# Norm 2's scales, one weight chunk's rounding and the last product's columns: three reorderings in a decoder block

## The chip, the cores and the metric

The kernel runs on one core of a Trainium2 chip. The metric is the device time of one execution in microseconds (us); lower is better. Engine names are those of the profile: PE multiplies matrices (PEld loads its weights), DVE, ACT and POOL work element by element, and SP is the queue from which most DMAs are issued.

## The reference

One decoder block on 512 positions of width 1024. Two token mixers run side by side and are merged by gates; then comes a SwiGLU channel mixer and a final norm. The change touches what follows the merge:

```python
m = jax.nn.sigmoid(z_ga) * y_a + jax.nn.sigmoid(z_gb) * y_b
x = x + m @ w_mix_out[l]                       # 1024 x 1024

h = rmsnorm(x, norm2_g[l])                     # "norm 2"
x = x + (jax.nn.silu(h @ ffn_w1[l]) * (h @ ffn_w3[l])) @ ffn_w2[l]   # 1024 -> 2816 -> 1024
return rmsnorm(x, norm_f_g)                    # final norm
```

## The kernel before

**Numbers in two parts.** Every product is made of float32r parts: an operand is split into a rounded high part (a cast on ACT, L133) and the rest as a low part (a subtraction on DVE or POOL, L129). One product is three matmuls: high by high, high by low, low by high. This split of a weight is called its *rounding* here.

**Weight chunks.** Weights come in a fixed list of chunks of up to 128 x 1024 (`chunks`). `load_chunk` issues the chunk's DMAs into one of four `raw` buffers, `emit_chunk` rounds it into one of five `hl` buffers, and `weights(key, ahead)` emits the list up to `ahead` chunks behind the one that is asked for (`AHEAD` is 4). Around the change the list reads: the last chunks of the mix matrix, then fb11_1, fb21_1, fb11_2, fb21_2, ft4_1, ft4_2 (quarters of ffn_w1 and ffn_w3 for the column pairs 1 and 2), then f1_0, f3_0, f1_1, f3_1 (pair 0, whole). The profile drops the numbers: fb11_2 is written from `raw_fb` to `hl_fb`, f3_0 from `raw_f` to `hl_f`.

**Seven products in place of eight.** The class `Sevenfold` multiplies by the mix matrix and by ffn_w2 in quarters, with sums of quarters in place of some of them. The output x is held as four row tiles of 128 positions, each in two halves of 512 columns: `x2[t][h]`. PE sums in PSUM banks (`bank`, `bank2`: 128 x 512 float32 each), r1, r2, r5 and r7, and `plus(t, h, b)` adds a bank to a half on DVE (L940). The steps at the end are `second` (products of the last index k; row tiles 0 and 1 are complete behind them) and `third(i, ks)` (the last products, into bank r1[i] once more, which complete row tile 2 + i).

**The end of the mix, `mix_end`.** Inside `manual_schedule` PE, ACT and DVE run in the order of the code. After `second` come six additions, then norm 2 for tiles 0 and 1: `rstd_begin` has squared the first-known half on ACT, `rstd_end` squares the other half, takes the root (ACT L562) and the reciprocal (DVE L563), and `scaled(t, h)` multiplies both halves by it (DVE L1100, into `xs`) and stores x to DRAM on the SP queue (`x2k`). PE then works off `third` in portions and, between them, transposes the scaled tiles in blocks of 128 columns (`turn_half`, PE L579): block c takes columns 128c to 128c + 127 of two row tiles, so blocks 0 to 3 need first halves only and blocks 4 to 7 second halves only. ACT makes the high part of each turned block (L582, h20h to h27h) and DVE the low part (L583). On the SP queue and POOL, pieces of later weights are loaded (L383), summed (`piece_sums`, L129 and L394) and stored (L398) in the same stretch.

**The start of the channel mixer.** The products for pairs 1 and 2 begin (PE L1211) on the turned columns of tiles 0 and 1. Tiles 2 and 3 are normalised meanwhile (`scaled(t, 0)`) and turned in between, blocks 4 to 7 first, and `fourth` multiplies by ft4 (L1255). When the last block is turned, banks are copied out (ACT L1241, L1259), the two SiLUs of `first` run (ACT L1221), and four more chunks are emitted.

**The end, `out_end`.** ffn_w2's product ends in the same steps. Each row tile is finished by the final norm: squares and a root on ACT (L555, L561, L562), a reciprocal on DVE, the multiplication by the norm's weights (DVE L1378), and the scale (L1388, L1390 on DVE, L1392 on ACT), then the DMAs to the output (L1395). For tiles 2 and 3 the last five products of `third` run in between (`rest`).

Outside `manual_schedule` the compiler's scheduler places instructions; `tc.issue_after(x)` holds them behind x.

Of the kernel before, what the change touches and what calls it, by code (L numbers as in the profile page):

```python
# [13 lines left out]
P = 128  # L14
# [82 lines left out]
def tile_block(ctx, tc, a, out):  # L97
# [449 lines left out]
    stats = consts.tile([P, 3 * NT, 3], F32, name="stats")  # L547
# [11 lines left out]
    def rstd_end(begun, half, junk):  # L559
        ss, r = begun  # L560
        act.activation(junk, half, AF.Square, accum_out=ss[:, 1:2])  # L561
        newest["root"] = act.activation(r, ss[:, 1:2], AF.Sqrt, scale=1.0 / D, bias=ss[:, 0:1]).ins  # L562
        vec.reciprocal(r, r)  # L563
        return r
# [385 lines left out]
    class Sevenfold:  # L950
# [35 lines left out]
        def product(self, banks, i, x_, w_, start, stop, again=False):  # L986

            (xh, xl), (wh, wl) = x_, w_
            ts = slice(i * P, (i + 1) * P)
            for n, (l_, r_) in enumerate(((xh, wh), (xh, wl), (xl, wh))):  # L990
                pe.matmul(banks[i], l_[:, ts], r_, start=start and n == 0, stop=stop and n == 2, skip_group_check=again)  # L991

        def run(self, sums, begun, end):
# [40 lines left out]
            def third(i, ks):  # L1034
                for k in ks:
                    self.product(r1, i, quarter(late[k][1], HI), *get(k, "t4"), False, k == kh - 1, True)

            for k in range(kh - 1):
                second(k, *get(k, "b22", "t2", "t3"))
                split_late()  # L1040
                if k == 0:
                    for i in range(2):
                        plus(i, 1, r5[i])
                        plus(2 + i, 1, r5[i])

            act.activation(warm, late[-1][1][0][:, :1].bitcast(F32), AF.Sqrt, scale=0.0, bias=eps_t)
            last = get(kh - 1, "b22", "t2", "t3", ahead=AHEAD - 1)
# [32 lines left out]
    def mix_end(second, plus, r1, r2, r7, third):  # L1080
        made = []

# [14 lines left out]
        def scaled(t, h):  # L1097
            r = rstd_end(begun[t], x2[t][h], sc[t][h])
            for i in range(2):
                newest["scaled"] = vec.tensor_scalar(out=sc[t][i], in0=x2[t][i], scalar1=r, scalar2=None, op0=ALU.mult).ins  # L1100
                nc.sync.dma_start(x2_kept[t][i][:, :], x2[t][i])


        with tc.manual_schedule(engines={ET.PE, ET.Activation, ET.DVE}):
# [7 lines left out]
            for t in range(2):  # L1112
                scaled(t, 1)
# [3 lines left out]
            for q in range(2):  # L1117
                turn_half("th", xs, "norm2_g", h2p, 0, [bank, bank2], range(4 * q, 4 * q + 4))
                for i in range(2):
                    third(i, [2 + q])  # L1120
# [14 lines left out]
            for t in (2, 3):  # L1135
                scaled(t, 0)
# [184 lines left out]
    with tc.issue_after(turned[0]), tc.issue_after(turned[1]):  # L1321
        for b in begun.values():
            b.first()
        emit_to(emitted[0] + 4)
        f_inputs()
# [46 lines left out]
    def finish(t, rest=None):  # L1372
# [13 lines left out]
        r = rstd_of([x2[t][h], x2[t][1 - h]], [bank2(f"jk{t}{i}") for i in range(2)], between)  # L1386

        vec.tensor_scalar(out=o[1 - h], in0=o[1 - h], scalar1=r, scalar2=None, op0=ALU.mult)  # L1388
        if t == 2:
            vec.tensor_scalar(out=o[h], in0=o[h], scalar1=r, scalar2=None, op0=ALU.mult)  # L1390
        else:
            act.activation(o[h], o[h], AF.Copy, scale=r)  # L1392

        for i in (1 - h, h):
            (nc.scalar if t == 3 and i == h else nc.sync).dma_start(o_nat[:, t, i * T : (i + 1) * T], o[i])  # L1395

    def out_end(second, plus, r1, r2, r7, third):
        kh, hold = outq.kh, 5
        second()
        for i in range(2):  # L1400
            plus(i, 1, r1[i])
            plus(i, 1, r2[i])
            plus(2 + i, 1, r1[i])
# [10 lines left out]
        for i in range(2):  # L1414

            def rest():
                third(i, range(kh - hold, kh))
                plus(2 + i, 0, r1[i])

            finish(2 + i, rest)  # L1420
# [35 lines left out]
```

## Time and profile before

| what | value |
|---|---|
| median of 3 runs | 799.59 us (799.19 to 799.9) |
| the profiled execution | 798.86 us |
| its span (first to last instruction) | 797.0 us |
| mean granted clock of PE | 0.998 |
| DMA | 188.13 MB, mean 236 GB/s |
| POOL busy | 360.2 us |
| PE's starts: mix product's end to first product of the channel mixer | 447 to 459 us |
| PE's last matmul begins | 789.91 us |

The span starts with the first instruction of the program. A row of a timeline gives the start, the time from the first start to the last end of the merged instructions, the engine, the line, the operation, output <- inputs, the shape and the count; in square brackets stands how long the engine was idle before it and what ended that. Starts of successive rows on PE and DVE overlap the ends of the earlier ones, since both engines are pipelined; how fast work goes through is read from the distance of the starts. A row of the waits gives the total, the number and the longest one. A row of the chain that ended last gives the start, the time, the engine and the line.

### The profile page before, as it was taken

The numbers are of one execution on the slowest core, as the hardware profiler recorded it, in microseconds if no ns is written. First come the engines' busy times: TensorE is split into PE (matmuls) and PEld (weight loads), VectorE is DVE, ScalarE is ACT, GpSimd is POOL, SyncE is SP. The second block draws the span as 40 slices with busy tenths as digits, with TensorE's granted clock in tenths as the row PEclk, the third lists the DMA queues.
The fourth block names the chain that finished last, engine by engine and source line by source line (L and its number), as shares of the span: only waits on it lengthen the run. The fifth ranks groups of instructions, "written<-read, shape, count | busy, mean of one in ns | idle before, by whom it ended". The sixth has DMA issues, their size and how long they took to land.

```text
span 797.0 us, 12582 instructions
## 1 busy us (share of the span) xinstructions
PE 786.5 (99%) x4374; PEld 688.8 (86%) x4374; DVE 695.8 (87%) x1097; ACT 472.6 (59%) x674; POOL 360.2 (45%) x347
## 2 busy tenths in 40 slices
PE   8999999999999999999999999999999999999996
PEld 7988888888888888888888797999999999888885
DVE  5799999999998997985899868898877798999956
ACT  7446688777679665562326466544455555556843
POOL 2576778788869988853350482113222221000000
PEclk9999999999999999999999999999999999999999
DMA  7746566577776786979987987588998898878652
GB/s 222 190 122 177 157 191 201 174 236 236 195 246 212 249 264 195 295 236 295 296 293 240 275 259 217 157 267 269 343 309 291 297 325 299 235 235 269 197 169 105
DMA packets 181074, 188.13 MB, mean 236 GB/s; under 512 B 14119, under 2 KB 142035, under 8 KB 181011
## 3 DMA queue, kind: packets, MB, share of 16 engines
q1 hardware_dynamic: 172195, 156.66, 63.8%
q0 software_dynamic: 8672, 30.41, 11.2%
q8 instruction: 34, 0.56, 0.3%
q10 hardware_dynamic: 144, 0.26, 0.1%
q14 instruction: 29, 0.24, 0.1%
HBM read 145.48 MB, written 38.80 MB: 231 GB/s over the span
## 4 chain that ended last, share of the span: by engine, by line
PE 95%; DVE 2%; ACT 1%; DMA 0%; issue 0%; SPq 0%; DVEq 0%
PE z L539 35%; PE fr L1211 24%; PE or L991 13%; PE yb L539 7%; PE ya L539 5%; PE mxr L991 4%; PE g L860 3%; PE f L539 2%; PE fr L1255 1%; DMA x<-in_x_dram 0%; DVE x L940 0%; PE z L632 0%; PE th L579 0%; PE tx L590 0%; DVE xs L1100 0%
## 5 line engine op out<-in xcount | busy, mean ns | idle before, releaser
L733 DVE SCALAR_TENSOR_TENSOR cv<-u,par,cv 128x511 f32<-128x511 f32 (+17 forms) x240 | 162.6, 728 | 1.1 <-ACT cv L730 0.9
L129 POOL TENSOR_TENSOR hl_in<-raw_in,hl_in 128x1024 fp32r<-128x1024 f32 x51 | 123.3, 2422 | 64.2 <-ACT hl_in L133 43.4
L129 POOL TENSOR_TENSOR fws<-fws 128x256 f32<-128x256 f32 x120 | 104.7, 875 | 75.1 <-DMA fws<-in_ffn_w_dram 69.5
L398 POOL DMA_DIRECT2D ot<-fwso x21 | 15.3, 731 | 166.1 <-DVE fwso L129 158.8
L1211 PE MATMUL fr<-hs_0h,hl_ft 128*128 128x256 f32 x320 | 59.2, 283 | 0.0
L133 ACT CAST hl_in<-raw_in 128x1024 fp32r<-128x1024 f32 x51 | 53.1, 1043 | 2.2 <-DMA raw_in<-in_w_in_dram 1.0
L129 DVE TENSOR_TENSOR hl_ft<-raw_ft,hl_ft 128x1024 fp32r<-128x1024 f32 x39 | 47.5, 1219 | 4.7 <-ACT hl_ft L133 4.7
L129 DVE TENSOR_TENSOR hl_fb<-raw_fb,hl_fb 128x1024 fp32r<-128x1024 f32 x30 | 36.9, 1231 | 15.9 <-ACT hl_fb L133 15.9
L1211 PEld LDWEIGHTS fr<-hs_0h,hl_ft 128*128 128x128 f32 x320 | 50.6, 192 | 0.0
L133 ACT CAST hl_ft<-raw_ft 128x1024 fp32r<-128x1024 f32 x40 | 41.6, 1047 | 12.4 <-PE fr L1211 9.2
L133 ACT CAST hl_fb<-raw_fb 128x1024 fp32r<-128x1024 f32 x30 | 31.5, 1050 | 24.4 <-PE fr L1211 11.6
L1211 PE MATMUL fr<-hs_0l,hl_ft 128*128 128x256 f32 x160 | 45.3, 283 | 0.0
L539 PE MATMUL z<-h10h,hl_in 128*128 128x512 f32 (+1 forms) x110 | 41.4, 378 | 0.0
L539 PE MATMUL z<-h11h,hl_in 128*128 128x512 f32 (+1 forms) x110 | 41.1, 376 | 0.0
L539 PE MATMUL z<-h17h,hl_in 128*128 128x512 f32 (+1 forms) x110 | 41.1, 376 | 0.0
L539 PE MATMUL z<-h13h,hl_in 128*128 128x512 f32 (+1 forms) x110 | 41.1, 376 | 0.0
L539 PE MATMUL z<-h14h,hl_in 128*128 128x512 f32 (+1 forms) x110 | 41.1, 376 | 0.0
L539 PE MATMUL z<-h15h,hl_in 128*128 128x512 f32 (+1 forms) x110 | 41.1, 376 | 0.0
L539 PE MATMUL z<-h16h,hl_in 128*128 128x512 f32 (+1 forms) x110 | 41.1, 376 | 0.0
L539 PE MATMUL z<-h12h,hl_in 128*128 128x512 f32 (+1 forms) x110 | 41.1, 375 | 0.0
L133 ACT CAST hl_ob<-raw_ob 128x1024 fp32r<-128x1024 f32 (+1 forms) x23 | 23.4, 1016 | 23.9 <-PE or L991 12.1
L394 POOL TENSOR_TENSOR fws<-fws 128x256 f32<-128x256 f32 x40 | 32.5, 813 | 2.8
(962 smaller groups left out, 2639.2 us busy)
## 6 DMA issues: line engine op xcount, KB each, us to landing
raw_in<-in_w_in_dram SPq DMA_DIRECT2D x52, 512.0 KB
fws<-in_ffn_w_dram SPq DMA_DIRECT2D x80, 256.0 KB
raw_ft<-fs SPq DMA_DIRECT2D x34, 512.0 KB
fs<-fws SPq DMA_DIRECT2D x23, 512.0 KB
ot<-fwso POOLq DMA_DIRECT2D x21, 512.0 KB, 5.8
fwso<-in_ffn_w_dram POOLq DMA_DIRECT2D x40, 256.0 KB, 7.3
fs<-fws POOLq DMA_DIRECT2D x17, 512.0 KB, 5.0
raw_ob<-in_ffn_w_dram SPq DMA_DIRECT2D x33, 256.0 KB
```

The lines of the kernel that those rows point to most:

```text
L129: return eng.tensor_tensor(out=o, in0=x, in1=y, op=ALU.subtract)
L133: copy(h, full)
L394: eng.tensor_tensor(out=q11, in0=q22, in1=q11, op=ALU.add)
L398: return queue.dma_start(dest, raw.rearrange("p (m n) -> p m n", m=dest.shape[1]))
L539: pe.matmul(ps, l, r, start=i == 0, stop=i == n - 1)
L733: vec.scalar_tensor_tensor(out=acc[c][:, s:], in0=u[c][:, : T - s], scalar=dw(c, s), in1=acc[c][:, s:], op0=ALU.mult, op1=ALU.add)
L860: pe.matmul(ps, l, r, start=k == 0, stop=k == len(mms) - 1)
L991: pe.matmul(banks[i], l_[:, ts], r_, start=start and n == 0, stop=stop and n == 2, skip_group_check=again)
L1211: pe.matmul(ps[:, HALVES[i]], lw[:, c, :], rx_, start=not (again or i or c or m), stop=bool(i and c == 3 and m == 2), skip_group_check=True,)
L1255: pe.matmul(self.r4[:, HALVES[i]], lw, rx_, start=not (i or c or m), stop=bool(i and c == 3 and m == 2), skip_group_check=True)
```

## The change

Five edits:

1. In the mix product the weight chunks are asked for one less ahead, so that fb11_2 is not rounded there. Its load is issued at the start of `mix_end`, ahead of the piece loads, and its rounding stands behind the first four transposed blocks.
2. `scaled` takes two row tiles. Both get their first half scaled, then both their second half. The second tile's root and reciprocal stand ahead of its first half's scale, as before.
3. Of the four chunks that were emitted behind the two SiLUs of `first`, one (f3_0) is emitted ahead of them.
4. In `out_end` the two additions from bank r1[i] follow each other, ahead of the one from r2[i].
5. Row tile 3 is finished by a function of its own. The last two of its five products (k = 9, 10) run in two parts of 256 columns, each followed by its own addition; the squares and the multiplication of that half go in two parts too, and the sums of squares meet through a small DVE operation and the bias of the root. The second scale of tile 2 moves from DVE to ACT.

```diff
-    stats = consts.tile([P, 3 * NT, 3], F32, name="stats")
+    stats = consts.tile([P, 3 * NT, 4], F32, name="stats")
...
-        def product(self, banks, i, x_, w_, start, stop, again=False):
+        def product(self, banks, i, x_, w_, start, stop, again=False, cs=slice(0, T)):
...
-                pe.matmul(banks[i], l_[:, ts], r_, start=start and n == 0, stop=stop and n == 2, skip_group_check=again)
+                pe.matmul(banks[i][:, cs], l_[:, ts], r_[:, cs], start=start and n == 0, stop=stop and n == 2, skip_group_check=again)
...
-            def third(i, ks):
+            def third(i, ks, cs=slice(0, T)):
                 for k in ks:
-                    self.product(r1, i, quarter(late[k][1], HI), *get(k, "t4"), False, k == kh - 1, True)
+                    self.product(r1, i, quarter(late[k][1], HI), *get(k, "t4"), False, k == kh - 1, True, cs)
 
             for k in range(kh - 1):
-                second(k, *get(k, "b22", "t2", "t3"))
+                second(k, *get(k, "b22", "t2", "t3", ahead=AHEAD - (k == kh - 2 and not self.lag)))
...
-            last = get(kh - 1, "b22", "t2", "t3", ahead=AHEAD - 1)
+            last = get(kh - 1, "b22", "t2", "t3", ahead=AHEAD - (1 if self.lag else 2))
...
     def mix_end(second, plus, r1, r2, r7, third):
         made = []
+        load_chunk(emitted[0])
...
-        def scaled(t, h):
-            r = rstd_end(begun[t], x2[t][h], sc[t][h])
+        def scaled(ts, h):
+
+            rs = []
             for i in range(2):
-                newest["scaled"] = vec.tensor_scalar(out=sc[t][i], in0=x2[t][i], scalar1=r, scalar2=None, op0=ALU.mult).ins
-                nc.sync.dma_start(x2_kept[t][i][:, :], x2[t][i])
+                for n, t in enumerate(ts):
+                    if not i:
+                        rs.append(rstd_end(begun[t], x2[t][h], sc[t][h]))
+                    newest["scaled"] = vec.tensor_scalar(out=sc[t][i], in0=x2[t][i], scalar1=rs[n], scalar2=None, op0=ALU.mult).ins
+                    nc.sync.dma_start(x2_kept[t][i][:, :], x2[t][i])
...
-            for t in range(2):
-                scaled(t, 1)
+            scaled((0, 1), 1)
...
                 turn_half("th", xs, "norm2_g", h2p, 0, [bank, bank2], range(4 * q, 4 * q + 4))
+
+                if not q:
+                    emit_to(emitted[0] + 1)
                 for i in range(2):
                     third(i, [2 + q])
...
-            for t in (2, 3):
-                scaled(t, 0)
+            scaled((2, 3), 0)
...
     with tc.issue_after(turned[0]), tc.issue_after(turned[1]):
+        emit_to(emitted[0] + 1)
         for b in begun.values():
             b.first()
-        emit_to(emitted[0] + 4)
+        emit_to(emitted[0] + 3)
         f_inputs()
...
         r = rstd_of([x2[t][h], x2[t][1 - h]], [bank2(f"jk{t}{i}") for i in range(2)], between)
-
+        store(t, o, r, h)
+
+    def store(t, o, r, h):
         vec.tensor_scalar(out=o[1 - h], in0=o[1 - h], scalar1=r, scalar2=None, op0=ALU.mult)
-        if t == 2:
-            vec.tensor_scalar(out=o[h], in0=o[h], scalar1=r, scalar2=None, op0=ALU.mult)
-        else:
-            act.activation(o[h], o[h], AF.Copy, scale=r)
+        act.activation(o[h], o[h], AF.Copy, scale=r)
...
+    def finish_last(bank_of, products, last_products):
+
+        x_, o, junk = x2[3], [shortt(f"of3{i}") for i in range(2)], bank2("jk30")
+        (ss, r), i = rstd_begin(x_[1], bank2("jk31")), n_stats[0] - 1
+        more = stats[:, i, 3:4]
+        vec.tensor_tensor(out=o[1], in0=x_[1], in1=gf[1], op=ALU.mult)
+        products()
+        with tc.manual_schedule(engines={ET.Activation, ET.DVE}):
+            for cs in HALVES:
+                last_products(cs)
+                add(x_[0][:, cs], bank_of[:, cs], x_[0][:, cs])
+            act.activation(junk[:, LO], x_[0][:, LO], AF.Square, accum_out=ss[:, 1:2])
+            act.activation(junk[:, HI], x_[0][:, HI], AF.Square, accum_out=more)
+            vec.tensor_tensor(out=o[0][:, LO], in0=x_[0][:, LO], in1=gf[0][:, LO], op=ALU.mult)
+            vec.tensor_scalar(out=ss[:, 0:1], in0=ss[:, 1:2], scalar1=1.0 / D, scalar2=ss[:, 0:1], op0=ALU.mult, op1=ALU.add)
+            vec.tensor_tensor(out=o[0][:, HI], in0=x_[0][:, HI], in1=gf[0][:, HI], op=ALU.mult)
+            act.activation(r, more, AF.Sqrt, scale=1.0 / D, bias=ss[:, 0:1])
+            vec.reciprocal(r, r)
+            store(3, o, r, 1)
...
         for i in range(2):
             plus(i, 1, r1[i])
+            plus(2 + i, 1, r1[i])
             plus(i, 1, r2[i])
-            plus(2 + i, 1, r1[i])
...
-        for i in range(2):
-
-            def rest():
-                third(i, range(kh - hold, kh))
-                plus(2 + i, 0, r1[i])
-
-            finish(2 + i, rest)
+
+        def rest():
+            third(0, range(kh - hold, kh))
+            plus(2, 0, r1[0])
+
+        finish(2, rest)
+        finish_last(r1[1], lambda: third(1, range(kh - hold, kh - 2)), lambda cs: third(1, range(kh - 2, kh), cs))
```

## The prediction

> **What bounds the kernel now.** The page's busy shares come first, then the list of who waited for whom on PE, then the chain that ended last.
>
> ```profile
> PE 786.5 (99%) x4374; PEld 688.8 (86%) x4374; DVE 695.8 (87%) x1097; ACT 472.6 (59%) x674; POOL 360.2 (45%) x347
> ```
>
> ```profile
> PE tx L590 <- DVE x L610: 1.6, 2, 1.3
> ...
> PE th L579 <- DVE xs L1100: 0.6, 1, 0.6
> ```
>
> ```profile
> 509.61 175.68 PE fr L1211 x1464
> 685.29 101.85 PE or L991 x448
> ```
>
> PE works 786.5 us of the 797.0 us span, and after the start it waits for another engine by name only once: 0.6 us at norm 2's transposes (L579). The chain gives the two paces I use: 101.85 us / 448 = 0.227 us per 512-column matmul and 175.68 / 1464 = 0.120 us per 256-column one. Where two starts of the PE timeline stand further apart than that, PE stood still, listed or not. Such places near the change are at 454, 484 and 775 us, and after PE's last matmul there is the tail. So the prize is small: every term below is under 1 us, 0.2% of this kernel is 1.6 us, and 0.2% is also about what a measurement of it can tell from no change.
>
> **Part 1: the first scales and the moved rounding.** Timelines of PE, then DVE, then ACT:
>
> ```profile
> 447.49 0.39 PE L991 MATMUL mxr<-hl_mxt,mxvb3l 128*128 128x512 f32 x1
> ...
> 453.94 0.27 PE L579 MATMUL th<-ident,xs 128*128 128x128 f32 x1
> 454.79 0.98 PE L579 MATMUL th<-ident,xs 128*128 128x128 f32 x7 [0.58 <-DVE xs L1100]
> ```
>
> ```profile
> 446.97 1.44 DVE L129 TENSOR_TENSOR hl_fb<-raw_fb,hl_fb 128x1024 fp32r<-128x1024 f32 x1 [1.43 <-ACT hl_fb L133]
> 448.33 4.06 DVE L940 TENSOR_TENSOR x<-mxr,x 128x512 f32<-128x512 f32 x6
> ...
> 452.50 1.65 DVE L1100 TENSOR_SCALAR xs<-x,stats 128x512 f32<-128x512 f32 x2
> ...
> 454.25 0.88 DVE L1100 TENSOR_SCALAR xs<-x,stats 128x512 f32<-128x512 f32 x2
> ```
>
> ```profile
> 452.58 0.29 ACT L562 ACTIVATE stats<-stats 128x1 f32<-128x1 f32 x1
> ...
> 456.24 0.48 ACT L582 ACTIVATE h23h<-th,par 128x256 fp32r<-128x256 f32 x1
> ```
>
> Reading: the first transposes need the first halves of both row tiles. PE turned tile 0's at 453.94 and stood until tile 1's first half was scaled (454.25 plus half of 0.88). Two things made that late. The low part of chunk fb11_2 (1.44 us) sat ahead of the six additions, so they began at 448.33 although the first sum was ready at 447.49 + 0.39 = 447.88. And tile 0's second half was scaled before tile 1's first: the two took 1.65 us together, against 0.88 for the next two.
>
> After the change the additions begin at 447.9 and end 0.4 us earlier, at about 452.0 (448.33 + 4.06 - 0.4). The square root of tile 1 (452.58 + 0.29) comes as much earlier, at 452.5. Tile 0's first half is scaled from 452.1, and tile 1's at 452.6 to 453.1 at the pace of 0.44 each (0.88 / 2), or by about 454.0 if the two run as slowly as the 1.65 us pair. PE gets to the transposes at 453.94. So its stall goes nearly whole: 454.79 - 453.94 = 0.85, of which the transpose itself keeps about 0.1. Some 0.05 comes from smoother starts. **Term: -0.8 us**, -0.55 if the scales are slow.
>
> The moved chunk's load goes to the same place of the SP queue:
>
> ```profile
> 439.07 1.21 SPq L355 DMA_DIRECT2D raw_fb<-in_ffn_w_dram  x2
> 440.38 2.25 SPq L383 DMA_DIRECT2D fws<-in_ffn_w_dram  x4
> ...
> 450.67 3.58 SPq L398 DMA_DIRECT2D fs<-fws  x2
> ```
>
> ```profile
> 446.58 2.42 POOL L129 TENSOR_TENSOR fws<-fws 128x256 f32<-128x256 f32 x2 [32.01 <-DMA fws<-in_ffn_w_dram]
> ```
>
> Its two issues stood ahead of the piece loads. The new code loads it just ahead of the same piece loads, so DMA changes nothing: a nothing whose cover is that the load precedes L398's stores, which block SP until POOL's sums are done. The four piece loads landed some 4 us after their last issue (446.58 against 440.38 + 2.25). The rounding comes about 16 us after the load, so it should not wait.
>
> **Part 2: where the rounding goes, and the second pair of scales.** DVE, ACT, PE:
>
> ```profile
> 457.93 0.48 DVE L583 SCALAR_TENSOR_TENSOR h24l<-th,par,h24h 128x256 fp32r<-128x256 f32 x1 [0.60 <-ACT h24h L582]
> ...
> 466.38 0.88 DVE L1100 TENSOR_SCALAR xs<-x,stats 128x512 f32<-128x512 f32 x2
> ...
> 467.37 0.88 DVE L1100 TENSOR_SCALAR xs<-x,stats 128x512 f32<-128x512 f32 x2
> 468.17 1.22 DVE L129 TENSOR_TENSOR hl_ft<-raw_ft,hl_ft 128x1024 fp32r<-128x1024 f32 x1
> ```
>
> ```profile
> 466.79 0.29 ACT L562 ACTIVATE stats<-stats 128x1 f32<-128x1 f32 x1
> ```
>
> ```profile
> 469.32 0.60 PE L579 MATMUL th<-ident,xs 128*128 128x128 f32 x4
> ```
>
> The rounding is queued on ACT behind h23h and on DVE behind its low part, and ahead of h24 to h27 on both. With PE 0.8 us earlier, h23h is through at 455.9 (456.24 + 0.48 - 0.8), the cast takes 1.0 (2.94 / 3 in part 3's row at 481.35) and the subtraction 1.22 (468.17) to 1.44 (446.97), so h24's low part starts at 458.1 to 458.35 where it started at 457.93: DVE gains nothing of PE's 0.8 and is 0.15 to 0.4 late. I take 0.2. The four low parts at 0.48 or less are done by 460.1. PE asks for them 60 matmuls ahead of the transposes at 469.32, so at 469.32 - 60 x 0.120 - 0.8 = 461.3, and nothing shows yet. But all DVE work up to the scales of tiles 2 and 3 keeps that delay. There the new order costs more: half 1's transposes come first (c = 4, 5 need second halves), and the new code scales the first halves of both tiles first. Before, tile 2's second half filled the time in which tile 3's root (466.79 + 0.29 = 467.08) was made. Now the reciprocal waits for that root, and the last scale ends about 0.35 later: 467.37 + 0.88 + 0.35 + 0.2 = 468.8. PE gets to tile 3's transpose at 469.32 + 0.1 - 0.8 = 468.6. **Term: +0.2 us** (0.1 to 0.4). DVE sets this point, so the slow scales of part 1 would cost less here.
>
> **Part 3: one rounding ahead of the SiLUs.** PE, ACT, DVE:
>
> ```profile
> 484.29 0.39 PE L539 MATMUL f<-h20l,hl_f 128*128 128x512 f32 x1
> 484.79 0.50 PE L539 MATMUL f<-h20h,hl_f 128*128 128x512 f32 x1
> 485.12 0.40 PE L539 MATMUL f<-h21h,hl_f 128*128 128x512 f32 x1
> ```
>
> ```profile
> 479.43 1.28 ACT L1221 ACT_TABLE_LOAD   x1
> ...
> 481.35 2.94 ACT L133 CAST hl_f<-raw_f 128x1024 fp32r<-128x1024 f32 x3
> ```
>
> ```profile
> 483.52 3.48 DVE L129 TENSOR_TENSOR hl_f<-raw_f,hl_f 128x1024 fp32r<-128x1024 f32 x3
> ```
>
> PE waited for the low part of f3_0 (its DVE subtraction from 483.52): 0.50 - 0.23 = 0.27, and 0.33 - 0.23 = 0.10 on the next start. The chunk's cast moves from 481.35 to about 479.4, ahead of the table load, and its subtraction to about 480.5, done by 481.8. The SiLUs come 1 us later; what they feed is not read for many microseconds. **Term: -0.37 us.**
>
> **Part 4: order of the last additions.** PE and DVE:
>
> ```profile
> 774.68 0.39 PE L991 MATMUL or<-hl_ot,oeb10l 128*128 128x512 f32 x1
> 775.06 0.70 PE L991 MATMUL or<-hl_ot,ovb0h 128*128 128x512 f32 x2
> ```
>
> ```profile
> 773.63 3.07 DVE L940 TENSOR_TENSOR x2b<-or,x2b 128x512 f32<-128x512 f32 x5
> ```
>
> PE restarts on bank r1 once its second reader is done, the second of these five additions (about 774.9). Put next to the first reader it ends about 774.3. PE lost 0.38 - 0.23 = 0.15 and 0.08 on the next start. **Term: -0.2 us.**
>
> **Part 5: the tail.** PE, DVE, ACT, and a 256-column addition elsewhere:
>
> ```profile
> 789.91 0.39 PE L991 MATMUL or<-hl_ot,ovb10l 128*128 128x512 f32 x1
> ```
>
> ```profile
> 789.64 0.49 DVE L1388 TENSOR_SCALAR of<-of,stats 128x512 f32<-128x512 f32 x1
> 790.05 0.48 DVE L1390 TENSOR_SCALAR of<-of,stats 128x512 f32<-128x512 f32 x1
> 790.44 0.68 DVE L940 TENSOR_TENSOR x2b<-or,x2b 128x512 f32<-128x512 f32 x1
> ```
>
> ```profile
> 791.16 0.60 ACT L561 ACTIVATE jk<-x2b 128x512 f32<-128x512 f32 x1 [1.75 <-DVE x2b L940]
> ...
> 791.92 0.29 ACT L562 ACTIVATE stats<-stats 128x1 f32<-128x1 f32 x1
> ```
>
> ```profile
> 425.90 0.42 DVE L940 TENSOR_TENSOR mxs<-mxv 128x256 f32<-128x256 f32 x1
> ```
>
> Old path: last matmul ends 790.30, addition 790.44 to 791.12, square, root at 791.92. The change makes six 512-column matmuls into twelve of 256: 12 x 0.120 - 6 x 0.227 = +0.08. It moves L1390's scale to ACT, so DVE is free at 790.05. A half addition takes 0.42 and a half square about 0.2 less than a whole one (0.60; between none and 0.3 less).
>
> What the trace doesn't show is PE writing one column half of a bank while DVE reads the other; both parts lie in one bank. Bound below: they run side by side. Then the last matmul ends 790.38, addition 790.42 to 790.84, square; from there to the root it took 791.92 - 791.16 = 0.76, now 0.56, so root at about 791.44: -0.48. Bound above: the second part waits for the first addition. Part one ends at 789.7, its addition runs behind L1388 at 790.05 to 790.47, PE restarts at 790.55, needs 0.6 + 0.08 for a restart and 0.28 for the last one: 791.5. Addition to 791.97, root at 792.57: +0.65 (+0.3 if DVE is free at 789.7). The nearest row is 775.06, where PE started on a bank only once DVE had read it out. It has the same columns, which is why the other bound stays. I take the wait. **Term: +0.6 us.** The Trainium skill (PSUM — Partial Sum Buffer, "PSUM bank collisions raise a hardware error") says that two engines may not touch one bank in the same quadrant at once, disjoint columns included. By that rule the wait must be there; no row here shows it.
>
> **Sum.** -0.8 + 0.2 - 0.37 - 0.2 + 0.6 = -0.57 us. The durations are those of a profiled execution of 798.86 us (797.0 us span and 1.86 around it); the median shown is 799.59 and the difference is taken from it: **799.0 us**. Behind 485 us the weights are rounded up to four chunks ahead (AHEAD; the cast row of part 3 holds three at once), so I let PE keep what it gained.
>
> **Rivals.**
> 1. *The two column parts overlap.* For it: the parts are different addresses. Against it: the row at 775.06. The tail then gives -0.48, the sum -1.65: **797.9 us**.
> 2. *The moved load comes late: slower.* It decides at SP's L398 stores. If the load is issued behind them (454.3 in place of 439.07), it lands about 458.3 to 460. The cast holds ACT and the subtraction holds DVE in front of h24 to h27; those end about 464 in place of 460, PE waits 2.6 us at 461.3, and DVE, 4 us late, makes it wait again at the second transposes, about 3.3 us behind the old time: +3.3 - 0.37 - 0.2 + 0.6 = +3.3, **802.9 us**. Below some 8 us of delay of the load nothing shows. Against it: the code loads ahead of the pieces.
> 3. *It doesn't do what it says.* The second transposes eat the whole 0.8 (DVE 0.6 later than I think, by POOL's additions beside the rounding) and the tail waits: -0.37 - 0.2 + 0.6 = 0.0: **799.6 us**.
>
> **How the numbers follow.** Chances: forecast 0.47 (798.5 to 799.5 by the bounds of its terms), rival 1 0.33 (797.4 to 798.3), rival 2 0.1, rival 3 0.1. Faster by over 0.2% means under 798.0, most of rival 1 and nothing else: 0.24. Slower means over 801.2: rival 2 and a little of 3: 0.12. Within: 0.64. The range from 797.6 to 800.1 leaves out rival 2 and the edges of 1 and 3.
>
> **What would show it.** Right: no wait of L579 on xs in the list at 454; a short one near 468.7; hl_f's first subtraction near 480.5 and no 0.50 start near 484; a gap of about 0.8 us in PE's last twelve matmuls with an addition in it. Wrong: no such gap (rival 1); hl_fb's cast released by its DMA (rival 2); a wait of over 0.5 us at the second transposes (rival 3); or a new wait of PE between 485 and 774.

## The result and the profile after

| kernel | median, us | lowest to highest | runs |
|---|---|---|---|
| before | 799.61 | 799.05 to 800.41 | 6 |
| changed | 802.71 | 801.43 to 804.45 | 6 |

The ratio is 1.0038, with a 95% interval from 1.0025 to 1.0052: the changed kernel came out 3.1 us slower, where 0.6 us faster was forecast. Two repeats with 12 runs of the changed kernel each gave less (below): 1.0016 and 1.0006, and neither of their intervals excludes 1. (The ratios are estimates of their own, not the quotients of the two medians, which would be 1.0017 in the second repeat.) The profiled execution took 803.02 us with a span of 801.2 us, 4.26 us more than before (801.22 against 796.95 in the trace).

PE is nearly as full as it was by the first section of the page, and DVE has two more instructions that count as busy:

```profile
PE 788.5 (98%) x4380; PEld 691.0 (86%) x4380; DVE 697.4 (87%) x1099; ACT 473.7 (59%) x677; POOL 361.0 (45%) x347
```

The list of who waited for whom on PE (total, times, longest, in us) has lost L579 and gained three rows:

```profile
PE mxr L991 <- DVE x L940: 1.6, 2, 1.4
...
PE or L991 <- DVE x2b L940: 0.9, 1, 0.9
PE fr L1217 <- DVE h24l L583: 0.5, 1, 0.5
```

The second new row is part 5's wait, which was forecast. The third is a wait that the prediction said would not come. The first lies at 437 us, ahead of the first instruction that the change touches, as does a start that is 1.1 us late.

To see where 4.26 us came from, take each matmul that both programs have and subtract its start before from its start after. This offset is constant while PE runs at its pace, and jumps where PE gains or loses. Its jumps, in us by the time before, for this profile and two more of the changed kernel (labels as in the experiments):

| place | cause | first profile | e1_after | e4_after | forecast |
|---|---|---|---|---|---|
| start (to 430) | ahead of the change | +1.12 | -0.21 | +1.20 | 0 |
| 437 | ahead of the change: L991 on L940 | +2.15 | +0.04 | +1.07 | 0 |
| 454 | part 1, L579 | -0.89 | -0.91 | -0.91 | -0.8 |
| 459 | part 2, L1217 on h24l | +0.75 | +0.75 | +0.74 | 0 |
| 469 | part 2, second transposes | +0.30 | +0.29 | +0.33 | +0.2 |
| 485 | part 3 | -0.43 | -0.43 | -0.39 | -0.37 |
| 775 | part 4 | -0.27 | -0.27 | -0.27 | -0.2 |
| tail, to the last scale on ACT | part 5 | +0.68 | +0.68 | +0.68 | +0.6 |
| last scale to the end of the span | not foreseen | +0.86 | +0.85 | +0.86 | 0 |
| sum without the first two | | +1.00 | +0.96 | +1.03 | -0.57 |

So the change's own places repeat to 0.05 us each, their sum to 0.07, and they cost 1.0 us together. The first two places differ by 3 us between executions of the same program. Two places make the difference between the forecast -0.57 and +1.00: 459 with 0.75 us and the end of the span with 0.86; the other five together are 0.04 us better than forecast. Below, "own" is this last sum: the difference of the spans less the offset that PE has at 445 us.

**The failed place, 459 us.** Before, the first product of the channel mixer follows the last one of the mix without a stop:

```profile
459.02 0.39 PE L991 MATMUL mxr<-mxt43h,mxvb3l 128*128 128x512 f32 x1
459.25 0.28 PE L1211 MATMUL fr<-h20h,hl_fb 128*128 128x256 f32 x1
```

Timelines of PE, ACT and DVE of the changed kernel follow; their times hold the 3.27 us of the first two places, less 0.9 on PE from 454 on:

```profile
456.88 0.39 PE L991 MATMUL mxr<-mxt41h,mxvb1l 128*128 128x512 f32 x1
457.11 1.03 PE L579 MATMUL th<-ident,xs 128*128 128x128 f32 x8
...
461.41 0.40 PE L991 MATMUL mxr<-mxt43h,mxvb3l 128*128 128x512 f32 x1
462.27 0.39 PE L1217 MATMUL fr<-h20h,hl_fb 128*128 128x256 f32 x1 [0.46 <-DVE h24l L583]
```

```profile
458.62 0.48 ACT L582 ACTIVATE h23h<-th,par 128x256 fp32r<-128x256 f32 x1
458.97 1.06 ACT L133 CAST hl_fb<-raw_fb 128x1024 fp32r<-128x1024 f32 x1
459.91 0.50 ACT L582 ACTIVATE h24h<-th,par 128x256 fp32r<-128x256 f32 x1
```

```profile
459.22 0.47 DVE L583 SCALAR_TENSOR_TENSOR h23l<-th,par,h23h 128x256 fp32r<-128x256 f32 x1
460.07 1.75 DVE L129 TENSOR_TENSOR hl_fb<-raw_fb,hl_fb 128x1024 fp32r<-128x1024 f32 x1 [0.37 <-ACT hl_fb L133]
461.74 0.47 DVE L583 SCALAR_TENSOR_TENSOR h24l<-th,par,h24h 128x256 fp32r<-128x256 f32 x1
```

The transposes now follow the matmul ahead of them without a stop (456.88, 457.11): part 1 did its work. Then the first product of the channel mixer, which reads h20h and hl_fb, waits for h24l. It doesn't read h24. What it needs is the PSUM bank in which block 4 was turned (by the code, blocks 0, 2, 4 and 6 take turns in two banks, and this product's sum comes next), and that bank is free only when DVE has made h24's low part from it. The moved rounding stands ahead of it, 1.75 us long, so h24l is done at 462.2 and PE starts 0.86 us after the matmul ahead instead of 0.23 us.

The rounding is that long because it runs into POOL's additions (L1078, which add the two parts of a turned block). One of them begins at 460.00, just ahead of it, and takes 0.74 us; the next takes 1.71. In all seven profiles with the moved rounding behind the first or the second group of blocks it is the same: 1.59 to 1.75 us. Where the rounding stood before, it took 1.22 to 1.23 us when POOL's addition began after it (e1_before, e1_tail, e2_scaled), 1.32 to 1.49 when that had begun 0.3 to 0.5 us earlier, and 1.73 to 1.80 when it had begun up to 0.1 us earlier (e3_best2, e1_stats). DVE's subtraction is longer by what is left of POOL's addition, less some 0.13 us.

**The tail.** PE, DVE and ACT of the changed kernel:

```profile
792.09 0.28 PE L991 MATMUL or<-hl_ot,ovb10l 128*128 128x256 f32 x1
793.24 0.51 PE L991 MATMUL or<-hl_ot,ovb9h 128*128 128x256 f32 x2 [0.87 <-DVE x2b L940]
```

```profile
792.37 0.49 DVE L1397 TENSOR_SCALAR of<-of,stats 128x512 f32<-128x512 f32 x1
792.77 0.42 DVE L940 TENSOR_TENSOR x2b<-or,x2b 128x256 f32<-128x256 f32 x1
794.26 0.42 DVE L940 TENSOR_TENSOR x2b<-or,x2b 128x256 f32<-128x256 f32 x1 [1.07 <-PE or L991]
```

```profile
795.84 0.72 ACT L1398 ACTIVATE of<-of,stats 128x512 f32<-128x512 f32 x1 [0.23 <-DVE stats L1420]
796.59 0.37 ACTq L1401 DMA_DIRECT2D out_dram<-of  x1
```

This is the upper bound of part 5 as it was worked out: the first part's addition runs behind DVE's scale (792.77 to 793.19), and PE goes on at 793.24. What was not foreseen comes behind it: from the last scale's start the span has 801.22 - 795.84 = 5.38 us to go, where the kernel before has 796.95 - 792.44 = 4.51: 0.86 us more before rounding.

### The profile page after: what moved, and what is told of

Read it like the earlier page. It is cut to its first block, busy times and chain, and to the rows that moved or that the text cites. A ratio compares the mean times of both kernels' runs of the same rounds, so it can differ in the third digit from the quotient of the medians.

```text
span 801.2 us, 12601 instructions
## 1 busy us (share of the span) xinstructions
PE 788.5 (98%) x4380; PEld 691.0 (86%) x4380; DVE 697.4 (87%) x1099; ACT 473.7 (59%) x677; POOL 361.0 (45%) x347
## 4 chain that ended last, share of the span: by engine, by line
PE 81%; DVE 9%; DMA 5%; issue 2%; ACT 2%; SPq 1%; DVEq 0%; ACTq 0%
PE z L539 35%; PE fr L1217 23%; PE or L991 13%; PE g L860 3%; PE f L539 3%; PE mxr L991 2%; DMA mxws<-in_w_mix_out_dram 2%; DMA raw_lo<-in_lru_w_out_dram 1%; PE fr L1261 1%; PE yb L539 1%; DVE hl_mxb L129 1%; DVE mxws L129 1%; DMA x<-in_x_dram 1%; DVE hl_co L129 1%; DVE u L777 1%
## 5 line engine op out<-in xcount | busy, mean ns | idle before, releaser
L129 POOL TENSOR_TENSOR hl_in<-raw_in,hl_in 128x1024 fp32r<-128x1024 f32 x51 | 123.2, 2422 | 64.9 <-ACT hl_in L133 41.9
L129 POOL TENSOR_TENSOR fws<-fws 128x256 f32<-128x256 f32 x120 | 103.7, 867 | 76.9 <-DMA fws<-in_ffn_w_dram 71.0
L1217 PE MATMUL fr<-hs_0h,hl_ft 128*128 128x256 f32 x320 | 59.2, 283 | 0.0
L129 DVE TENSOR_TENSOR hl_ft<-raw_ft,hl_ft 128x1024 fp32r<-128x1024 f32 x39 | 47.5, 1217 | 4.9 <-ACT hl_ft L133 4.9
L1217 PEld LDWEIGHTS fr<-hs_0h,hl_ft 128*128 128x128 f32 x320 | 50.6, 192 | 0.0
L129 DVE TENSOR_TENSOR hl_fb<-raw_fb,hl_fb 128x1024 fp32r<-128x1024 f32 x30 | 37.5, 1252 | 14.4 <-ACT hl_fb L133 14.4
L1217 PE MATMUL fr<-hs_0l,hl_ft 128*128 128x256 f32 x160 | 45.3, 283 | 0.0
```

Source lines behind the costliest of these rows:

```text
L129: return eng.tensor_tensor(out=o, in0=x, in1=y, op=ALU.subtract)
L1217: pe.matmul(ps[:, HALVES[i]], lw[:, c, :], rx_, start=not (again or i or c or m), stop=bool(i and c == 3 and m == 2), skip_group_check=True,)
```

## The experiments

"Own" and the places are read as in the table above, each from one profile; ratios are to the kernel before, timed alongside.

**1. The kernel before again, the changed kernel again, the wider tile, the tail alone.** Theory A: what lies outside the change's places belongs to single executions. Theory B: it comes with the changed kernel. Form C of B: it comes with the addresses, since `stats` grew.

e1_before: no edit.

> The kernel before, unchanged, timed against itself: a control. Theory A (the change's own steps cost about +0.2 us in the trace: -0.8 +0.7 +0.2 -0.35 -0.3 +0.7; the other 4 us of the profiled difference, +1.1 at the start, +2.1 in the wait at L940 near 437 and +0.8 in the last output transfers, are a matter of one execution) expects a ratio of 1.000 with single times spread over 2 to 3 us, and a profile in which the start or the wait at 437 may differ from the first one. Theory B (these 4 us come with the changed kernel whenever it runs) expects 1.000 with a spread of 1.4 us, and the same start and the same absence of a wait at 437 as in the first profile.

e1_after: no edit to the changed kernel.

> The changed kernel again, unchanged. Theory A expects the start and the wait of L991 on x's additions near 437 to differ from the first profile of it, and a ratio nearer to 1.000 than 1.004. Theory B expects 1.003 to 1.005 again, with the wait near 437 of some 2 us and the later start again in the profile.

e1_stats, the kernel before with

```diff
-    stats = consts.tile([P, 3 * NT, 3], F32, name="stats")
+    stats = consts.tile([P, 3 * NT, 4], F32, name="stats")
```

> The kernel before with one edit: the stats tile has 4 columns in place of 3, which nothing reads; every tile allocated behind it moves by 48 bytes per partition. Theory B in its form C (the new addresses set the start and the wait at 437) expects about +3 us, ratio 1.004, and in the profile the wait of L991 on x near 437. Theory A, and theory B in any other form (the length of the program, the order of the later code), expect 1.000 and no such wait.

e1_tail, the kernel before with part 5 of the change's diff alone (`finish_last`, `store`, `cs`, and the wider `stats`).

> The kernel before with part 5 alone (the last tile's product in two column parts, its new end, stats 4 columns wide). Theory A expects +0.7 us, ratio 1.0008: PE's second column part waits for the first part's addition, which itself waits for DVE's scale of the tile ahead. Form C expects +0.7 and some 3 us beside it, 1.0045. The first rival of the prediction (the column parts overlap) would give -0.5 us; the profile of the changed kernel speaks against it.

| kernel | median, us (before: 799.94) | ratio, 95% | start | 437 | tail | last scale to end | own |
|---|---|---|---|---|---|---|---|
| e1_before | 800.22 | 1.0002 (0.9989 to 1.0016) | -0.15 | +0.16 | 0.00 | +0.01 | +0.02 |
| e1_after | 801.15 | 1.0016 (0.9996 to 1.0036) | -0.21 | +0.04 | +0.68 | +0.85 | +0.96 |
| e1_stats | 799.82 | 1.0000 (0.9985 to 1.0014) | +1.32 | +0.10 | 0.00 | -0.01 | +0.33 |
| e1_tail | 800.37 | 1.0000 (0.9985 to 1.0015) | -0.34 | +0.45 | +0.68 | +0.23 | +0.98 |

The changed kernel ran here without the late start and without the wait at 437: B falls for these two, and C falls with e1_stats: the ratio is 1.0000, and there is no wait at 437. (Its profile has a late start of 1.32 us, as e3_34 has with `stats` as it was; its 0.33 is a late start of PE at 452.5, which experiment 3 explains.) A falls for the third: the 0.85 us behind the last scale came again with the changed kernel, so it is no chance. In the tail alone it is 0.23, so the code of the tail isn't the reason for the rest. That 0.23 isn't in the transfers: their last packet ends 2.87 us after the last scale's start, as in the kernel before, and 1.87 us ahead of the end of the span in place of 1.65. Why is open.

The transfers of the last 4 us explain it. The view of DMA traffic has 40 slices (a strip of busy tenths, one of GB/s, the queues with their packets, MB and share). The changed kernel from 796 to 800.5 us, 0.1125 us a slice:

```profile
DMA  0000000000499999999989620100000000000000
GB/s 0 0 0 0 0 0 0 0 0 0 127 328 419 382 364 400 383 346 419 419 328 419 237 55 0 18 0 18 36 18 18 0 0 0 0 0 0 0 0 0
...
q14 instruction: 1, 0.01, 0.4%
```

and the kernel before from 792.5 to 796.5 us, 0.1 us a slice:

```profile
DMA  0000000000003699999999999961000000000000
GB/s 0 0 0 0 0 0 0 0 0 0 0 0 102 225 410 369 389 410 451 348 348 369 389 348 451 389 226 21 0 0 0 0 0 0 0 0 0 0 0 0
...
q10 hardware_dynamic: 144, 0.26, 17.4%
```

Before, the two last outputs run at nearly 400 GB/s to their end, and no packet of queue 14 is in the window; the fetch comes at 798.3, behind the end of the span. After, a fetch of instructions (queue 14, one packet of 8 KB, at 798.2) falls among them, and behind the full stretch single packets trickle on for 0.8 us: 18 GB/s x 0.1125 us is 2 KB, one packet per slice. In the trace each of these packets starts as the one ahead of it ends, from 798.60 to 799.49, while all others are done by 798.70: they look like the share of a single DMA engine. That it is the engine which served the fetch is an inference, as the trace doesn't say which engine moved a packet, and why a fetch of 0.31 us costs 0.8 is open; that the fetch is the cause is tested next.

**2. Whose fetch it is, and where the rounding belongs.** DVE has 1343 instructions of all kinds in the trace of before, 1345 in e1_tail and 1346 in the changed kernel. Theory D: DVE's stream reaches its next block of 8 KB just ahead of the end, and a few instructions decide. Theory E: the step that failed is part 2, and what it lost hangs on where the rounding stands.

e2_before_pad3, the kernel before with

```diff
     n_stats = [0]
+    for _ in range(3):
+        vec.memset(stats[:, 0, 2:3], 0.0)
```

> The kernel before with three more 128x1 memsets on DVE in its first microseconds, which nothing reads; nothing else. Theory D: in both profiles of the changed kernel one fetch of 8 KB of instructions (queue 14) runs 1.6 us after the last output transfer is issued, among that transfer's packets, and the last two outputs land 3.2 and 3.4 us after their issue in place of 2.0 and 2.5; in the kernel before the same fetch comes behind the end. It is DVE's stream that decides it: the changed kernel has 1346 instructions on DVE, the one before 1343. D expects that three more bring the fetch before the end here too, the landing of the last output 0.7 us later, +0.7 us in all. The rival (the late landing comes from the new code of the tail) expects 0.0 and the fetch behind the end as before.

e2_after_pad24, the changed kernel with the same loop, 24 times.

> The changed kernel with 24 more such memsets on DVE at its start. Theory D expects that DVE's last fetch comes well ahead of the last output's packets, so that the last two outputs land 2.0 and 2.5 us after their issue again: 0.7 us less than the changed kernel in the same place, and about +0.3 us against the kernel before. The rival expects the landing at 3.2 and 3.4 us still, and +1.0 us against the kernel before.

e2_late, the changed kernel without part 5 and with

```diff
-                if not q:
+                if q:
                     emit_to(emitted[0] + 1)
```

> Parts 1 to 4 without part 5, and the moved rounding one group further back: behind h24 to h27 (both groups of transposed blocks) on ACT and DVE. Theory E (the step that failed is part 2: PE's first matmul of b0's half asks for h24's low part at 459, not at 461.3, since its bank is that of the transposed block) expects no wait of L1217 on h24l, so that the 0.8 us won at 454 are kept to the second transposes: -0.8 +0.2 to +0.6 there (the rounding now ends later and may hold the scales of tiles 2 and 3), -0.35 and -0.3 after, in all -0.8 to -1.3 us. The rival (PE waits at 459 for something else that moved, the load or POOL's sums) expects the 0.6 us lost again at 459.

e2_scaled, the kernel before with edit 2 of the list of edits alone (`scaled` takes two tiles).

> Only the order of the scales is changed: first halves of both row tiles first, the rounding of fb11_2 where it stood in the kernel before. Theory E expects that half of the stall at 454 goes (-0.4 us: the additions begin late as before, but tile 1's first half is scaled 0.4 us earlier), that nothing is lost at 459, and +0.2 us at the second transposes: -0.2 us at 470. A rival, that the scales' order alone brings the 0.8, expects -0.8 at 454 and that the rounding need not have been moved.

| kernel | median, us (before: 799.58) | ratio, 95% | start | 437 | 454 | 459 | 469 | last scale to end | own |
|---|---|---|---|---|---|---|---|---|---|
| e2_before_pad3 | 801.43 | 1.0021 (1.0009 to 1.0034) | +0.20 | +3.49 | +0.05 | 0.00 | 0.00 | +0.86 | +0.92 |
| e2_after_pad24 | 801.14 | 1.0023 (1.0006 to 1.0041) | +0.31 | +2.49 | -0.91 | +0.75 | +0.29 | 0.00 | +0.14 |
| e2_late | 798.70 | 0.9984 (0.9970 to 0.9998) | +0.77 | 0.00 | -0.90 | +0.01 | +1.11 | 0.00 | -0.46 |
| e2_scaled | one run, 799.25 | | +0.06 | +1.09 | -0.81 | 0.00 | 0.00 | +0.01 | -0.74 |

Theory D holds both ways, by the places. Three memsets that do nothing bring the fetch and its trickle into the kernel before; here is its DMA traffic from 796.5 to 800.5 us:

```profile
DMA  0000000000599999999998994001001000000000
GB/s 0 0 0 0 0 0 0 0 0 0 164 328 369 471 410 348 348 349 389 410 451 328 348 369 123 0 0 20 0 20 41 20 20 0 0 0 0 0 0 0
...
q14 instruction: 1, 0.01, 0.5%
```

In the changed kernel 24 of them move the fetch to 783.5, and its last stretch is clean (795.5 to 799.5 us; queue 14 isn't in it):

```profile
DMA  0000000000007999999999999920000000000000
GB/s 0 0 0 0 0 0 0 0 0 0 0 0 225 328 451 410 348 389 389 390 389 389 348 369 389 348 82 0 0 0 0 0 0 0 0 0 0 0 0 0
```

The change of own agrees: +0.92 for three memsets, and 1.00 - 0.14 = 0.86 back for 24. The median of e2_after_pad24 doesn't show that gain (1.0023, as with the fetch in e2_before_pad3, 1.0021); both padded kernels had 2.5 to 3.5 us of the wait at 437 in their profiles, and the kernel before with its memsets ahead of everything has it too:

```profile
PE mxr L993 <- DVE x L942: 2.9, 2, 1.6
```

Theory E is half right. With the rounding behind both groups of blocks (e2_late) nothing waits at 459, as it said. But then all of the 0.9 us and more is lost at the second transposes. DVE and the list of waits of e2_late:

```profile
468.83 0.16 DVE L563 RECIPROCAL stats<-stats 128x1 f32<-128x1 f32 x1 [0.26 <-ACT stats L562]
469.03 1.28 DVE L1105 TENSOR_SCALAR xs<-x,stats 128x512 f32<-128x512 f32 x3
```

```profile
PE th L579 <- DVE xs L1105: 0.6, 1, 0.6
```

And e2_scaled goes against E's number: the order of the scales alone, with the rounding where it always was, brings -0.81 us and loses nothing after. Its PE and DVE:

```profile
454.75 0.39 PE L991 MATMUL mxr<-mxt41h,mxvb1l 128*128 128x512 f32 x1
454.99 1.12 PE L579 MATMUL th<-ident,xs 128*128 128x128 f32 x8
```

```profile
453.42 0.77 DVE L1103 TENSOR_SCALAR xs<-x,stats 128x512 f32<-128x512 f32 x1
454.11 0.15 DVE L563 RECIPROCAL stats<-stats 128x1 f32<-128x1 f32 x1
454.30 1.56 DVE L1103 TENSOR_SCALAR xs<-x,stats 128x512 f32<-128x512 f32 x3
```

Tile 1's first half is scaled from 454.30, one third of 1.56 us, while PE turns tile 0's blocks from 454.99: it is in time with the rounding still ahead of the additions. So moving the rounding bought 0.1 us in this execution (-0.81 against -0.9), and cost what 459 and 469 show. It buys more where the rounding in its old place is slow, as experiment 3 shows.

**3. The sum of what helps, and a bank of its own for the second column part.**

e3_best1, the kernel e2_scaled with parts 3 and 4.

> The order of the scales, part 3 and part 4; the rounding of fb11_2 and its load where they stood in the kernel before, and its tail. Theory E (the order alone won 0.7 us at 454 and lost nothing after) expects -0.7 -0.35 -0.25 = -1.3 us, ratio 0.9984, with no wait of L1217 on h24l and none of L579 over 0.3 us. The rival (moving the rounding was needed; the one look at the order alone owed its 0.7 us to a late start of that execution's sums) expects -0.4 at 454, 0.2 to 0.5 us lost at the second transposes, and -0.6 us in all.

e3_best2, e3_best1 with the changed kernel's tail (and 24 memsets as above), and

```diff
-            for cs in HALVES:
-                last_products(cs)
-                add(x_[0][:, cs], bank_of[:, cs], x_[0][:, cs])
+            last_products(LO)
+            add(x_[0], bank_of, x_[0])
+            last_products(HI, [None, other])
+            add(x_[0][:, HI], other[:, HI], x_[0][:, HI])
```

> The kernel e3_best1 with the changed kernel's tail, but the second column part's six matmuls write another PSUM bank (that of tile 2's product, free by then), from zero; DVE adds the whole first bank, then the other's second half. 24 small memsets on DVE at the start keep the fetch of instructions away from the end. Theory F (the wait in part 5 is for the bank: the first part's addition reads the bank that the second part goes on writing) expects no gap in PE's last twelve matmuls, PE's end at the old time, the last addition done 0.4 us later than there at most and the last scale 0.1 us earlier than in the kernel before: -0.1 us for the tail, -1.4 us in all. The rival (the second part waits for something else: its operands or DVE's queue) expects the gap of 0.87 us again, and +0.6 us for the tail.

e3_norm2, the kernel before with parts 1 and 2.

> Parts 1 and 2 alone: the order of the scales, the load and the rounding moved behind the first group of transposed blocks. Theory E expects -0.8 us at 454, +0.6 at 459 (L1217 waits for h24l), +0.25 at 469: 0.0 to +0.1 us at 470. The rival (parts 1 and 2 of themselves gain, and what was lost at 459 came with parts 3 to 5) expects -0.6 us.

e3_34, the kernel before with parts 3 and 4.

> Parts 3 and 4 alone. All theories expect -0.35 us at 485 and -0.2 to -0.3 us at 775, nothing elsewhere; a different sign of either would undo the reading of the changed kernel's trace there.

| kernel | median, us (before: 799.87) | ratio, 95% | 454 | 459 | 469 | 485 | 775 | tail | own |
|---|---|---|---|---|---|---|---|---|---|
| e3_best1 | 798.43 | 0.9980 (0.9969 to 0.9991) | -0.69 | 0.00 | 0.00 | -0.42 | -0.27 | 0.00 | -1.39 |
| e3_best2 | 799.39 | 0.9996 (0.9973 to 1.0018) | -0.30 | 0.00 | 0.00 | -0.42 | -0.27 | -0.02 | -1.03 |
| e3_norm2 | one run, 799.63 | | -0.90 | +0.74 | +0.33 | +0.15 | 0.00 | 0.00 | +0.32 |
| e3_34 | one run, 799.55 | | -0.12 | 0.00 | 0.00 | -0.39 | -0.27 | 0.00 | -0.77 |

(The two places ahead of the change, start and 437, give +2.43 and 0.00, +2.30 and +0.83, -0.42 and +1.01, +1.19 and +0.29 us in these four profiles.)

e3_best1 came out as expected and beats both kernels: 1.4 us below the one before. In e3_best2 the gap in the last matmuls is gone; PE's second column part follows the first at its pace:

```profile
791.51 0.28 PE L993 MATMUL or<-hl_ot,ovb10l 128*128 128x256 f32 x1
791.63 0.40 PE L993 MATMUL or<-hl_ot,ovb9h 128*128 128x256 f32 x2
```

Theory F holds: the wait of part 5 was for the bank. The tail wins nothing by it, though, because DVE is next. Its scale of tile 2 and two additions stand in a row, from before PE's end to 793.4:

```profile
791.79 0.49 DVE L1394 TENSOR_SCALAR of<-of,stats 128x512 f32<-128x512 f32 x1
792.19 1.21 DVE L942 TENSOR_TENSOR x2b<-or,x2b 128x512 f32<-128x512 f32 x2
```

At 454, e3_best2 won 0.30 us where e3_best1 won 0.69. It lost the rest to a late start of PE at 452.5, as e1_stats did, and the traces say why: these are the two profiles in which the rounding, in its old place ahead of the additions, took 1.73 and 1.80 us. The additions came later by that, and PE started on the bank that they free 0.25 and 0.32 us late (in e1_stats the row names the addition, L940). In the other eight profiles with the old place, and in all seven with the rounding moved, this start is on time to 0.02 us. So moving the rounding is worth 0.1 us in e2_scaled's execution, 0.2 in e3_best1's and 0.6 in e3_best2's, against the 0.74 + 0.33 us that it cost in e3_norm2.

The Trainium skill (PSUM — Partial Sum Buffer, "PSUM bank collisions raise a hardware error") has the rule by which the wait of part 5 had to be there: two engines may not touch one bank in the same quadrant at once, other columns included. The traces agree as far as they go, 0.87 us of wait with one bank and none with two.

e3_norm2 puts parts 1 and 2 at +0.32 alone, and e3_34 shows the two small parts as forecast.

**4. The changed kernel a third time.** Open was whether the 2 us and more ahead of 445 us belong to it.

e4_after and e4_before: no edits.

> The changed kernel, a third time. If the 2 us belong to single executions: a ratio of 1.001 to 1.002, a lowest run about 1.0 us above the lowest run of the kernel before, and the profile with or without a wait near 437. If they belong to the kernel: 1.003 to 1.005 and the wait near 437 in the profile. In both cases L1217 waits 0.5 us for h24l, PE waits 0.9 us in the tail, and the last outputs land 3.2 and 3.4 us after their issue.

> The kernel before, a control. Ratio 1.000. If the 2 us belong to single executions, this kernel's runs spread over 3 us or more above their lowest, as the changed kernel's do; if not, over 1.5 us.

e4_parts1234, the changed kernel without part 5.

> The changed kernel without part 5: the old tail, stats 3 columns wide. The sum of the measured terms is -0.8 +0.7 +0.25 -0.35 -0.25 = -0.45 us, with no late fetch among the last outputs, as DVE has no more instructions than before: ratio 0.9994. If the terms hang together otherwise (the waits at 459 and 469 take more than the 0.8 won), 0.0 us or above.

| kernel | median, us (before: 799.63) | lowest to highest | ratio, 95% | start | 437 | own |
|---|---|---|---|---|---|---|
| e4_after | 800.96 | 799.65 to 804.33 | 1.0006 (0.9989 to 1.0024) | +1.20 | +1.07 | +1.03 |
| e4_before | 799.31 | 798.38 to 801.44 | 0.9987 (0.9973 to 1.0001) | +0.07 | +0.70 | +0.02 |
| e4_parts1234 | 798.67 | 798.27 to 804.51 | 0.9984 (0.9964 to 1.0005) | +0.16 | +0.08 | -0.50 |

The wait at 437 is in the kernel before, too (0.4 us in the list of e4_before):

```profile
PE mxr L991 <- DVE x L940: 0.4, 1, 0.4
```

Single runs of the kernel before reach 805 us here and 804 us in experiment 1. The lowest runs, which should have the least of this, stand apart by what the traces give: 799.54 against 798.65 us in experiment 1, 799.65 against 798.58 here, 0.9 and 1.1 us. Parts 1 to 4 add up to -0.50 us as expected.

## Why the prediction was wrong

Its sum was -0.57 us; the changed kernel's own places come to +1.0 us. Point by point:

- **Part 1** was right in size (-0.9 against -0.8) and half right in its reason. It named two things that made tile 1's first half late; e2_scaled shows that the order alone brings -0.81, and the rounding ahead of the additions counts for more only where it is slow (e3_best2).
- **Part 2 is the step that failed**: "PE asks for them 60 matmuls ahead of the transposes at 469.32, so at ... 461.3, and nothing shows yet". It asked who reads h24 to h27, and forgot who needs the bank that their makers read. PE asked at 459, and it cost +0.75. The step had h24l 0.15 to 0.4 us late; it came 3.81 us later by the trace (457.93 to 461.74), of which 3.27 are the late start and the wait at 437, so 0.5, as the rounding ran beside POOL's additions and took 1.75 us in place of 1.22 to 1.44. The missed wait is the larger mistake. PE, 0.9 us early, could have started at 459.25 - 0.89 = 458.36 of the old time, and it starts 0.53 us after h24l does; so h24l at the step's own 458.1 to 458.35 would have cost 0.3 to 0.5 us (an estimate from these rows), and the slower rounding adds most of the rest. The +0.2 at the second transposes was nearly right (+0.30), and again for another reason: e2_scaled has the new order and 0.00 there, so it is the rounding's delay, not the order.
- **Parts 3 and 4**: -0.41 and -0.27 against -0.37 and -0.2.
- **Part 5**: +0.68 against +0.6, its upper bound +0.65; rival 1 falls by the gap, and e3_best2 shows that the bank is the reason.
- **A term that was missing**: +0.86 us behind the last scale, the larger of the two misses. The working ended at the root and took the transfers behind it as unchanged, without a word on it. Nothing in the rows that it used spoke of the fetch.
- **Rivals**: the moved load did not come late (rival 2). Rival 3 was nearest: the gain of 454 was eaten, though mostly at 459, and its reason, POOL's additions beside the rounding, has a share in it. It had 799.6 us; with its tail and the fetch the own places give 799.59 + 1.0 = 800.6, above the range's 800.1.
- **The rest of the first result**, 3.1 us against 1.0, is the late start and the wait at 437. The two programs' instructions are the same up to there, engine by engine and in the same order; 17 profiles have the two together between -0.2 and +3.7 us, and 0 to 0.8 in the three of the kernel before. The wait comes when DVE has fallen behind PE, mostly between 345 and 425 us: in every profile it is DVE's delay at 425, over the kernel before, less some 0.65 us (2.81 gives 2.15 in the first one, 4.14 gives 3.49 in e2_before_pad3, 1.72 gives 1.09 in e2_scaled), or nothing. By the chain of the first profile DVE was held up there by transfers that landed late. Why an execution has it stays open, and so the cause of two thirds of the first result does. That the changed kernel has it more often is not excluded: its medians stand 3.1, 1.2 and 1.3 us above the kernel before, own being 1.0.

## What to carry to other kernels

When an instruction is put ahead of others on DVE or ACT, ask not only who reads their results, but also who waits for the buffer that they read: here a PSUM bank, wanted by a product that had nothing else to do with them. Try the halves of an edit alone: the reordering had nearly the whole gain, and the move beside it gave it back. When an instruction moves on one engine, look at what the other engines do at its new time: here it got 0.5 us longer beside POOL's additions. And where an effect of 1 us is looked for, compare traces place by place; the medians of 6 runs told three times that.

## What the runs showed of the hardware

- A fetch of 8 KB of instructions that lands among the last output's packets delays the end by 0.86 us, though it takes 0.3 us itself (0.4% of 16 engines in the window of 4.5 us): seven packets of 2 KB follow one after another when the others are done, as if one DMA engine had to finish alone. Three instructions more on DVE at the start of the program are enough to bring it there, 24 take it away again. The Trainium skill (Runtime: NRT & Kernel Launch, "Instruction fetch mechanics") calls the cost of such fetches mostly hidden; in the profiles here it shows only in the last 4 us, where the end waits for the transfers themselves.
- The same program's executions differ by 6 us and more (798.58 to 805.07 us for the kernel before in experiment 4). In the profiles up to 3.7 us of it are settled in the first 16 us and at one addition at 437 us.
- DVE's subtraction of two 128x1024 operands (L129) and POOL's additions get in each other's way: it takes 1.22 us when it starts first (e2_scaled, where POOL's addition beside it takes 1.78 in place of 0.74) and 1.73 to 1.80 us when POOL's addition has begun up to 0.1 us earlier (e3_best2, e1_stats, and the changed kernel).
